# Norms of queries and keys, the gate weight sums, a fold's bank and one tile's copy in a two-layer transformer kernel

## The chip, the cores and the metric

The kernel runs on one core of a Trainium2 chip. The metric is the time of one execution on the device in microseconds (us), as the median of several runs; lower is better. A profile of one execution gives the time of every instruction on the engines: PE is TensorE (matrix products, with PEld for loading its weights), DVE is VectorE, ACT is ScalarE, POOL is GpSimd, and SP issues the transfers (DMA).

## What is computed

A model of two layers on 512 latent tokens and 256 context tokens of width 1024, all in float32. Each layer has a mixer and a gated feed-forward block, and each is modulated by shift, scale and gate vectors that come from two condition vectors. Layer 0 mixes by grouped attention with normed and rotated queries and keys, layer 1 by a gated recurrence. The change lies in layer 0 before attention:

```python
mod_l = (jax.nn.silu(c) @ ada_w[i] + ada_b[i])[:, None, :]       # and mod_c from c_ctx
sh1_l, sc1_l, gt1_l, sh2_l, sc2_l, gt2_l = jnp.split(mod_l, 6, axis=-1)
hn_l = modulate(rms_norm(h, norm_mix_w[i]), sh1_l, sc1_l)         # h * (1 + scale) + shift

def rms_norm(x, w):
    xf = x.astype(jnp.float32)
    y = xf * lax.rsqrt(jnp.mean(xf * xf, axis=-1, keepdims=True) + NORM_EPS)
    return (y * w.astype(jnp.float32)).astype(x.dtype)

def attention_mixer(h_lat, h_ctx, w_qkv, q_norm, k_norm, w_o, rope, with_ctx_out):
    ...
    q_l = apply_axial_rope(queries(h_lat), rope)     # queries: (h @ w_q), rms_norm over the 64 of a head
    k_l, v_l = keys_values(h_lat)                    # keys: rms_norm in the same way
    k_l = apply_axial_rope(k_l, rope)
    k_c, v_c = keys_values(h_ctx)                    # context: normed, not rotated
    ...
    s = jnp.einsum('bkgqd,bksd->bkgqs', q, k) * (HEAD_DIM ** -0.5)   # softmax, times v, times w_o
```

There are 16 query heads and 4 key/value heads of 64. `gt1`, the gate of the mixer (chunk 2 of the six), multiplies the result of attention much later.

## The kernel before, in words

Every product is kept near float32 accuracy by splitting both sides into a high and a low part: `split` (L86 to L95) makes the high part with a cast on ACT (L88) and the low part with a subtraction on DVE (L93), and `mm3` (L114 to L118) does three products for one. Engines run their instructions strictly in the order of the program; the order on each engine is set by a scheduler at build time from the dependences, except for instructions that `pin` keeps in the order of the code.

The part of the program that matters, in order:

**Keys and values.** The normed input lies as eight tiles `xhT` (k = 0 to 7, 128 of the width each, 768 tokens). `kv_group` (L447 to L460) takes each k in turn: a modulate on DVE (L452), the split into `hnh` (ACT) and `hnl` (DVE), then 18 products of 128x512 into three pairs of PSUM banks `kv`. Between these products a filler (`gfill.step`, by the table `KV_STEPS`) puts steps of the modulation products: `ada_group` gives shift and scale in three groups, the last for k = 4 to 7, and `ada_chunk(2, ...)` (L201 to L209) then gives the gate `gt1` from eight blocks `adw` of 128x1024 weights, each one step of four products of 32x256 (`ada_mm`, L185). `ada_put` (L187 to L196) copies the sums to SBUF (`arows`, ACT), transposes them on PE into a bank `pta`, and adds the bias on DVE. The tiles `adw` share six buffers with earlier tiles, so an `adw` is fetched only when a buffer's last reader is done.

**Queries.** For each of four groups g of heads (the loop below `q_first`), two weight tiles `wq` are split (buffers for three high and three low parts), and three tiles of 256 tokens are computed, 48 products of 128x256 each, into one of four `q` banks. I call them tile 0 to tile 11 below. Behind the first three go the three key tiles. `qk_norm_rope` (L512 to L553) then norms and rotates each tile: the square on ACT (L521), the sum on DVE (L524), a scaling (L525), the root on ACT (L526), the reciprocal (L527) and one Newton step of four small operations (L528 to L531) on DVE, the product `qhat` (L533), the rotation on DVE (L543, L552) and POOL (L548), or for the context tile one product with the weight (L537). `k_first` makes two copies `kd` on DVE (L567) and the low part on POOL (L568); `q_first` makes `qd` on DVE (L596) and its low part on POOL (L597). Up to three tiles later PE transposes them into banks of 128x512 (`ptk` L578, `ptq` L603), of which there are three, and ACT copies them out; of the last four 64-row pieces of a key tile DVE copies two (L588). Between the tiles stand eight steps of `ada_chunk(3, ...)`, whose sums lie in a bank of their own, and whose transposes go to one of the three banks.

**Start of attention.** When the last query tile is done, its PSUM pool is closed and the banks become those of the scores `sc` (L656, L657): the first scores wait for the last reader of the `q` banks. PE also transposes the input once more (`rx`, L682) while the softmax of the first tiles begins.

## Time and profile before

| what | value |
|---|---|
| median of three runs (1820.36 to 1823.44) | 1823.32 us |
| the profiled execution's own time | 1821.68 us |
| span of its instructions | 1819.9 us |
| granted TensorE clock, mean over the span | 0.99 |
| first product of the keys and values | 28.24 us |
| first product of the queries (tile 0) | 77.08 us |
| first scores of attention | 179.16 us |

The times in the table's last three rows count from the start of the span. In the rows of the profile, a group of instructions has its line, engine and operation, out<-in by the program's names, the shape and the count; behind the bar stand busy time in us and the mean ns of one, then the idle time of the engine before them and what ended it. Rows of the timeline start with the start and the length in us. A window's row gives the busy time of each engine in that stretch, then the granted clock of PE as a share of full speed.

### The profile page before, as it was taken

To read this page: it belongs to the slowest core of one execution; us is meant where nothing else is said; L and a number is where in the kernel's file an instruction comes from. 1 tells how busy PE (TensorE), PEld (TensorE's weight loads), DVE (VectorE), ACT (ScalarE), POOL (GpSimd) and SP (SyncE) were. 2 spreads that over 40 slices of the span, in tenths; PEclk is the share of its full clock that TensorE was granted. 3 is DMA by queue.
4 is the path that set the end of the run, shared out by engine and by line. 5 is a ranking of instruction groups with operands and counts; after the bars stand their busy time and mean duration, and the time that the engine had idled before them with its cause. 6 is when DMAs were issued, how large, how long until landed. Compare 5 with 4: busy or idle time off the path is not lost.

```text
span 1819.9 us, 30696 instructions
## 1 busy us (share of the span) xinstructions
PE 1755.3 (96%) x11749; PEld 1606.9 (88%) x11749; DVE 1300.5 (71%) x2291; ACT 867.2 (48%) x1768; POOL 637.7 (35%) x583
## 2 busy tenths in 40 slices
PE   8988999999999999999999999999999899999998
PEld 6778678988899999999998999899898799999997
DVE  4587588888888878787865555665747758786764
ACT  4342787676642424333354443343434445554545
POOL 1244254345522304131414333144325544443420
PEclk9999999999999999999999999999999999999999
DMA  8533520002124243445331211222211223333322
GB/s 319 176 105 84 163 79 24 1 24 64 30 87 129 73 137 93 146 133 153 108 116 34 70 59 59 70 82 70 81 56 38 67 59 112 101 106 106 99 60 83
DMA packets 213459, 166.45 MB, mean 91 GB/s; under 512 B 7952, under 2 KB 190400, under 8 KB 213312
## 3 DMA queue, kind: packets, MB, share of 16 engines
q1 hardware_dynamic: 213024, 163.43, 29.2%
q8 instruction: 93, 1.52, 0.4%
q10 hardware_dynamic: 288, 1.05, 0.1%
q14 instruction: 54, 0.44, 0.1%
HBM read 162.36 MB, written 2.10 MB: 90 GB/s over the span
## 4 chain that ended last, share of the span: by engine, by line
PE 78%; DVE 9%; POOL 4%; ACT 4%; issue 2%; DMA 2%; SPq 0%; POOLq 0%; DVEq 0%; ACTq 0%
PE ffo L118 5%; PE ffo L116 5%; PE ffo L117 5%; PE x L116 4%; PE x L117 4%; PE x L118 4%; PE pt L714 3%; PE y L118 2%; PE y L116 2%; PE y L117 2%; PE lv L1643 2%; PE hz L116 2%; PE hz L117 2%; PE hz L118 2%; PE sc L656 2%
## 5 line engine op out<-in xcount | busy, mean ns | idle before, releaser
L1650 POOL TENSOR_TENSOR KD<-KD,tot 128x384 f32<-128x384 f32 x96 | 102.6, 1092 | 82.1 <-ACT kc L1633 78.4
L704 POOL TENSOR_SCALAR pf<-pf,st 128x768 f32<-128x768 f32 (+1 forms) x96 | 73.6, 769 | 128.1 <-DVE st L703 91.6
L687 DVE SCALAR_TENSOR_TENSOR hT<-ffo,modc,hT 128x512 f32<-128x512 f32 (+1 forms) x122 | 78.7, 649 | 48.2 <-PE ffo L118 48.2
L118 PE MATMUL ffo<-gh,wlo_w 128*128 128x512 f32 (+1 forms) x304 | 102.9, 339 | 0.0
L117 PE MATMUL ffo<-gl,whi_w 128*128 128x512 f32 (+1 forms) x304 | 102.4, 337 | 0.0
L116 PE MATMUL ffo<-gh,whi_w 128*128 128x512 f32 (+1 forms) x304 | 102.0, 338 | 0.0
L239 DVE SCALAR_TENSOR_TENSOR adacc<-adw,csil,adacc 128x512 f32<-128x512 f32 x98 | 84.5, 871 | 7.5 <-DMA adw<-in_ada_w_dram 7.4
L93 DVE TENSOR_TENSOR ptl<-pt,pth 128x384 fp32r<-128x384 f32 (+1 forms) x160 | 79.9, 524 | 12.4 <-ACT pth L88 11.2
L88 ACT CAST pth<-pt 128x384 fp32r<-128x384 f32 (+1 forms) x160 | 69.9, 461 | 34.3 <-PE pt L714 22.6
L700 DVE TENSOR_REDUCE st<-sc 128x1 f32<-128x768 f32 (+1 forms) x96 | 74.2, 773 | 15.3 <-PE sc L657 12.6
L702 ACT ACTIVATE pf<-sc,st 128x768 f32<-128x768 f32 (+1 forms) x96 | 73.4, 765 | 19.3 <-DVE st L700 18.4
L1650 DVE TENSOR_TENSOR QD<-QD,tot 128x256 f32<-128x256 f32 x96 | 52.0, 582 | 41.2 <-PE lv L1643 41.1
L1633 ACT COPY kc<-KD 128x256 f32<-128x256 f32 x112 | 43.4, 414 | 75.8 <-PE lv L1643 43.8
L714 PE MATMUL pt<-ident,pf 128*128 128x128 f32 x448 | 72.2, 275 | 5.2 <-DVE ptl L93 3.9
L116 PE MATMUL ffo<-gh,foh 128*128 128x512 f32 (+1 forms) x186 | 71.4, 384 | 0.0
L118 PE MATMUL ffo<-gh,fol 128*128 128x512 f32 (+1 forms) x186 | 70.8, 381 | 0.2 <-DVE fol L93 0.2
L117 PE MATMUL ffo<-gl,foh 128*128 128x512 f32 (+1 forms) x186 | 70.9, 381 | 0.0
L1709 POOL TENSOR_SCALAR oss<-oss 128x4 f32<-128x4 f32 (+1 forms) x9 | 4.7, 524 | 181.8 <-DVE oss L1708 181.7
L1643 PE MATMUL lv<-QD,kc 128*128 128x128 f32 x448 | 63.4, 286 | 4.5 <-DVE QD L1650 2.4
L1643 PEld LDWEIGHTS lv<-QD,kc 128*128 128x128 f32 x448 | 58.7, 192 | 8.8 <-ACT kc L1633 3.8
L714 PEld LDWEIGHTS pt<-ident,pf 128*128 128x128 f32 x448 | 51.2, 140 | 14.4 <-issue 6.4
L117 PEld LDWEIGHTS ffo<-gl,whi_w 128*128 128x128 f32 x304 | 57.4, 189 | 6.9
(1101 smaller groups left out, 6793.9 us busy)
## 6 DMA issues: line engine op xcount, KB each, us to landing
adw<-in_ada_w_dram SPq DMA_DIRECT2D x40, 512.0 KB, 4.7
adw<-in_ada_w_dram SPq DMA_DIRECT2D x80, 256.0 KB, 2.9
raw_hz<-in_hgrn_w_in_dram SPq DMA_DIRECT2D x14, 512.0 KB, 3.8
adr<-in_ada_w_dram SPq DMA_DIRECT2D x16, 256.0 KB, 4.7
adr<-in_ada_w_dram SPq DMA_DIRECT2D x8, 512.0 KB, 7.5
raw_wq<-in_attn_w_qkv_dram SPq DMA_DIRECT2D x8, 512.0 KB, 5.7
raw_wo<-in_attn_w_o_dram SPq DMA_DIRECT2D x8, 512.0 KB, 3.5
raw_hv<-in_hgrn_w_in_dram SPq DMA_DIRECT2D x8, 512.0 KB, 4.9
```

The lines of the kernel that those rows point to most:

```text
L93: m = (eng or DVE).tensor_tensor(lo, src, hi.bitcast(F32), op=ALU.subtract)
L116: PE.matmul(ps, ahi, bhi, start=first, stop=False, **kw)
L117: PE.matmul(ps, ahi, blo, start=False, stop=False, **kw)
L118: PE.matmul(ps, alo, bhi, start=False, stop=last, **kw)
L239: pin(DVE.scalar_tensor_tensor(a, raw, cc, a, op0=ALU.mult, op1=ALU.add))
L687: DVE.scalar_tensor_tensor(hT[o][:, a:e], ps, mcol(layer, ch, o, v), hT[o][:, a:e], op0=ALU.mult, op1=ALU.add)
L700: DVE.tensor_reduce(st3[:, 0:1], ps[:, :nk], op=ALU.max, axis=AX.X, negate=True)
L702: ACT.activation(pf, ps[:, :nk], AF.Exp, bias=st3[:, 0:1], accum_out=st3[:, 1:2])
L704: POOL.tensor_scalar(pf, pf, st3[:, 2:3], 1.0, op0=ALU.mult, op1=ALU.mult)
L714: PE.transpose(pt[:, i * P : (i + 1) * P], pf[:, (i0 + i) * P : (i0 + i + 1) * P], ident)
L1643: PE.matmul(ps[:, cs], kc[:, cs], mv, start=True, stop=True)
L1650: eng.tensor_tensor(view, view, f, op=ALU.mult)
```

## The change

It has six edits, all before attention.

1. **Gate weight sums.** Six of the eight blocks of the gate chunk are no longer multiplied on PE. DVE multiplies each block by the two condition values of its rows and adds it to two sums of 128x1024 (`asum`, twelve operations in fixed order); PE then multiplies the two remaining blocks, and adds each sum over its rows with a column of ones (`pick`), four steps in place of eight.
2. **Modulates.** Those of k = 4 to 7 no longer stand in `kv_group` but in the filler ahead of the sums; those of k = 6 and 7 move from DVE to ACT.
3. **Norm chain.** The scaling is folded into the root (`scale`, `bias`), and the Newton step takes three small operations for four, its constant -0.5/64 being folded into the norm weights (one more small POOL operation). Five DVE operations a tile are left of seven up to the factor `ss`, the sum and the reciprocal included.
4. **Keys.** The two copies `kd` and the two 64-row copies out of PSUM move from DVE to ACT.
5. **Fold.** The transposes of chunk 3 go to the free half of the bank that holds its sums.
6. **Last query tile.** DVE copies it from PSUM to SBUF (`qraw`) first; the norm chain reads the copy.

On SP the last two `adw` of the gate chunk come to stand behind one and two small transfers (`rows2`), ahead of which they stood, since their buffers are now released by the sums on DVE.

```diff
+ADA_SUMS = 6
...
-    def ada_put(pa, rows, dst, bias, nch, nk):
+    def ada_put(pa, rows, dst, bias, nch, nk, pt=None):
...
-        pt = bank("pta")
+        pt = bank("pta") if pt is None else pt
...
     def ada_chunk(ch, pa, rows, load):
+        pt = None if pa is None else pa[:, 256:512]
...
+    def ada_shared(ch, nsum):
+
+        pa = bank("pa")[:, 0:256]
+        sums = [stp.tile([P, D], F32, name=f"asum{v}") for v in range(2)]
...
+        for step in range(KT + 1):
+            if step < KT:
+                raws.append(xx_tile(f"adw{ch}{step}"))
+                dma(raws[-1], ada_w[0, step * P : (step + 1) * P, ch * D : (ch + 1) * D])
+            k = step - 1
+            if k >= nsum:
+                products(raws[k], cpad[:, k], k == nsum, False)
+            for v in range(2 if 0 <= k < nsum else 0):
+                cc = csil[:, v, k : k + 1]
+                if k == 0:
+                    pin(DVE.tensor_scalar(sums[v], raws[k], cc, None, op0=ALU.mult))
+                else:
+                    pin(DVE.scalar_tensor_tensor(sums[v], raws[k], cc, sums[v], op0=ALU.mult, op1=ALU.add))
+            yield
+        for v in range(2):
+            products(sums[v], pick[:, v], False, v == 1)
...
+    def first_modulate(k):
+        for v, a, e in SP2:
+            xs, sc, sh = xhT[k][:, a:e], a_c0[:, k, v : v + 1], mcol(0, 0, k, v)
+            if k < KT - 2:
+                DVE.tensor_scalar(xs, xs, sc, sh, op0=ALU.mult, op1=ALU.add)
+            else:
+                ACT.activation(xs, xs, AF.Identity, bias=sh, scale=sc)
+        split(hn_hi[k], hn_lo[k], xhT[k])
+
+    def last_modulates():
+        for k in range(KT // 2, KT):
+            first_modulate(k)
+        yield from ada_shared(2, ADA_SUMS)
...
-        DVE.tensor_scalar(ss, ss, 1.0 / HD, EPS, op0=ALU.mult, op1=ALU.add)
-        ACT.activation(sr, ss, AF.Sqrt)
+        ACT.activation(sr, ss, AF.Sqrt, bias=epst, scale=1.0 / HD)
         DVE.reciprocal(sr, sr)
         DVE.tensor_tensor(sa, sr, sr, op=ALU.mult)
-        DVE.tensor_tensor(sa, sa, ss, op=ALU.mult)
-        DVE.tensor_scalar(sa, sa, -0.5, 1.5, op0=ALU.mult, op1=ALU.add)
-        DVE.tensor_tensor(ss, sr, sa, op=ALU.mult)
+        DVE.scalar_tensor_tensor(sa, ss, HD * EPS, sa, op0=ALU.add, op1=ALU.mult)
+        DVE.scalar_tensor_tensor(ss, sa, -3.0 * HD, sr, op0=ALU.add, op1=ALU.mult)
...
-            DVE.tensor_copy(kd[:, :, :, i].rearrange("p t h d -> p (t h) d"), r.rearrange("p t h d -> p (t h) d"))
+            ACT.copy(kd[:, :, :, i].rearrange("p t h d -> p (t h) d"), r.rearrange("p t h d -> p (t h) d"))
...
-                    DVE.tensor_copy(dst[HD:P], pg[rows])
+                    ACT.copy(dst[HD:P], pg[rows])
...
+        if g == KVH - 1 and tp == 2:
+            raw = qst.tile([P, 512], F32, tag="kraw", bufs=2, name="qraw")
+            DVE.tensor_copy(raw, ps)
+            ps = raw
```

The order on three engines shows what moves; line numbers behind the edits are higher in the changed kernel (L93 is L94 there, L452 is L466). First DVE, from the split of k = 4 (`hnl_99`) to the first splits of the query weights. Before:

```order
L93 TENSOR_TENSOR hnl_99<-xhT_291,hnh_91 128x768
L93 TENSOR_TENSOR wlo_wkv_504<-raw_wkv_502,whi_wkv_503 128x1024
L93 TENSOR_TENSOR hnl_100<-xhT_300,hnh_92 128x768
L452 TENSOR_SCALAR xhT_309<-xhT_309,a_c_202,modc_82 128x256
L452 TENSOR_SCALAR xhT_318<-xhT_318,a_c_202,modc_82 128x512
L452 TENSOR_SCALAR xhT_318<-xhT_318,a_c_202,modc_82 128x256
L93 TENSOR_TENSOR hnl_101<-xhT_309,hnh_93 128x768
L93 TENSOR_TENSOR hnl_102<-xhT_318,hnh_94 128x768
L93 TENSOR_TENSOR wlo_wkv_572<-raw_wkv_570,whi_wkv_571 128x1024
L195 TENSOR_TENSOR modc_82<-pta,cols_80 128x16
L93 TENSOR_TENSOR wlo_wq_749<-raw_wq_747,whi_wq_748 128x1024
```

Of the changed kernel, with two pairs of sums left out at its end:

```order
L94 TENSOR_TENSOR hnl_99<-xhT_295,hnh_91 128x768
L94 TENSOR_TENSOR hnl_100<-xhT_304,hnh_92 128x768
L94 TENSOR_TENSOR hnl_101<-xhT_313,hnh_93 128x768
L94 TENSOR_TENSOR wlo_wkv_522<-raw_wkv_520,whi_wkv_521 128x1024
L94 TENSOR_TENSOR hnl_102<-xhT_322,hnh_94 128x768
L453 TENSOR_SCALAR asum_516<-adw_518,csil 128x1024
L453 TENSOR_SCALAR asum_517<-adw_518,csil 128x1024
L455 SCALAR_TENSOR_TENSOR asum_516<-adw_526,csil,asum_516 128x1024
L455 SCALAR_TENSOR_TENSOR asum_517<-adw_526,csil,asum_517 128x1024
L455 SCALAR_TENSOR_TENSOR asum_516<-adw_552,csil,asum_516 128x1024
L455 SCALAR_TENSOR_TENSOR asum_517<-adw_552,csil,asum_517 128x1024
L94 TENSOR_TENSOR wlo_wkv_584<-raw_wkv_582,whi_wkv_583 128x1024
```

The low weights of k = 4 and 5 (`wlo_wkv_522`) now stand behind three input splits, and the low weights of k = 6 and 7 behind six of the twelve sums.

Second ACT, from the copies of the first key tile out of PSUM (`kT`) to the root of tile 1 (its square reads `q_872`, in the changed kernel `q_871`). Before:

```order
L582 CAST kT<-ptk 128x2x256 x2
L587 CAST kT<-ptk 64x2x256
L521 ACTIVATE qrot<-q_872 128x512
L587 CAST kT<-ptk 64x2x256
L88 CAST whi_wq_1139<-raw_wq_1138 128x1024
L526 ACTIVATE ss<-ss 128x8
```

Of the changed kernel:

```order
L630 CAST kT<-ptk 128x2x256 x2
L635 CAST kT<-ptk 64x2x256
L636 CAST kT<-ptk 64x2x256
L635 CAST kT<-ptk 64x2x256
L636 CAST kT<-ptk 64x2x256
L615 CAST kd<-qrot 128x8x64 x2
L570 ACTIVATE qrot<-q_871 128x512
L89 CAST whi_wq_1130<-raw_wq_1129 128x1024
L575 ACTIVATE ss<-ss,epst 128x8
```

The square of tile 1 now stands behind the two `kd` copies of the second key tile.

Third PE at the start of attention, behind the transposes of tile 8 and 9. Before:

```order
L656 MATMUL sc<-kT,qT_705 128x512
L657 MATMUL sc<-kT,qT_705 128x512
L656 MATMUL sc<-kT,qT_705 128x256
L657 MATMUL sc<-kT,qT_705 128x256
L603 MATMUL ptq<-ident,qd 128x128 x8
L682 MATMUL rx_2040<-ident,hT_2004 128x128 x2
L603 MATMUL ptq<-ident,qd 128x128 x8
L682 MATMUL rx_2040<-ident,hT_2004 128x128 x4
L185 MATMUL pa<-adw_2120,cpad 32x256 x4
```

Of the changed kernel:

```order
L708 MATMUL sc<-kT,qT_707 128x512
L709 MATMUL sc<-kT,qT_707 128x512
L708 MATMUL sc<-kT,qT_707 128x256
L709 MATMUL sc<-kT,qT_707 128x256
L655 MATMUL ptq<-ident,qd 128x128 x8
L734 MATMUL rx_2014<-ident,hT_1978 128x128 x6
L708 MATMUL sc<-kT,qT_707 128x512
L709 MATMUL sc<-kT,qT_707 128x512
L708 MATMUL sc<-kT,qT_707 128x256
L709 MATMUL sc<-kT,qT_707 128x256
L655 MATMUL ptq<-ident,qd 128x128 x8
L186 MATMUL pa<-adw_2094,cpad 32x256 x4
```

The transposes of the last query tile (the second `ptq`) now stand behind all of `rx` and a second set of scores.

More of the change, by code (lines that the diff above doesn't have):

```diff
@@ L208, in ada_chunk @@
             yield
-        ada_put(pa, rows(), modc[0][:, ch : ch + 1], ada_bias(0, ch, 1), 1, KT)
+        ada_put(pa, rows(), modc[0][:, ch : ch + 1], ada_bias(0, ch, 1), 1, KT, pt)
     def ada_acc(layer, ch, nv, fp, wide):
@@ L423, with products @@
         gfill.add(ada_group(*g_))
-    gfill.add(ada_chunk(2, None, lambda: stp.tile([P, 256], F32, tag="arows", bufs=2, name="arows2"), xx_tile))
+    pick = stp.tile([P, 2, 32], F32, name="pick")
+    POOL.memset(pick, 0.0)
+    for v in range(2):
+        POOL.memset(pick[:, v, v : v + 1], 1.0)
+    def ada_shared(ch, nsum):
+        pa = bank("pa")[:, 0:256]
+        sums = [stp.tile([P, D], F32, name=f"asum{v}") for v in range(2)]
+        def products(m, col, start, stop):
+            m4 = m.rearrange("p (b j n) -> p b j n", b=2, j=4)
+            for j in range(4):
+                PE.matmul(pa[32 * j : 32 * (j + 1)], col, m4[:, :, j], start=start, stop=stop)
+        raws = []
+        for step in range(KT + 1):
[12 more added lines that the diff above has]
+            yield
+        for v in range(2):
+            products(sums[v], pick[:, v], False, v == 1)
+        rows = stp.tile([P, 256], F32, tag="arows", bufs=2, name="arows2")
+        ada_put(pa, rows, modc[0][:, ch : ch + 1], ada_bias(0, ch, 1), 1, KT)
+    def first_modulate(k):
[10 more added lines that the diff above has]
+        yield from ada_shared(2, ADA_SUMS)
+    gfill.add(last_modulates())
     gfill.step(4)
@@ L450, in kv_group @@
             k = k0 + j
-            for v, a, e in SP2:
-                DVE.tensor_scalar(xhT[k][:, a:e], xhT[k][:, a:e], a_c0[:, k, v : v + 1], mcol(0, 0, k, v),
-                                  op0=ALU.mult, op1=ALU.add)
-            split(hn_hi[k], hn_lo[k], xhT[k])
+            if k < KT // 2:
+                first_modulate(k)
             for t in range(NT):
@@ L496 @@
         dma(w, wsrc.to_broadcast([P, HD]))
[L497 to L498 removed]
+        POOL.tensor_scalar(w, w, -0.5 * sc / HD, 1.0, op0=ALU.mult, op1=ALU.mult)
         cw = qst.tile([P, NLT, HD], F32, name=f"cw{nm}")
```

2 lines of the change are left out of this document (removed).

## The prediction

> **What bounds the kernel now.** I read the page first:
>
> ```profile
> PE 1755.3 (96%) x11749; PEld 1606.9 (88%) x11749; DVE 1300.5 (71%) x2291; ACT 867.2 (48%) x1768; POOL 637.7 (35%) x583
> PE 78%; DVE 9%; POOL 4%; ACT 4%; issue 2%; DMA 2%; SPq 0%; POOLq 0%; DVEq 0%; ACTq 0%
> ```
>
> The first row says that PE is busy nearly always, the second that of the chain which ends last 22% is not PE. All six edits lie in the first 185 us, so I read only that stage: where PE waits from 77 to 185 us, and what clock PE was granted (windows; behind the five engines stand the clock, the DMA share and GB/s).
>
> ```profile
> PE q L117 <- DVE wlo_wq L93: 3.7, 2, 2.4
> PE sc L656 <- DVE qhat L533: 3.5, 1, 3.5
> PE pta L193 <- ACT kT L582: 3.3, 1, 3.3
> ```
>
> ```profile
> 118.00:122.00 4.00, 0.70 (x7) 0.46 (x5) 2.64 (x8) 1.28 (x4) 2.12 (x2) 0.89 0.50 191
> 122.00:128.00 6.00, 6.00 (x29) 6.00 (x30) 4.88 (x9) 1.05 (x3) 3.36 (x5) 0.50 0.01 1
> 133.00:136.00 3.00, 0.58 (x5) 0.48 (x5) 2.79 (x4) 0.32 (x1) 1.67 (x2) 1.00 0.00 0
> 175.00:179.00 4.00, 0.63 (x6) 0.39 (x4) 3.35 (x10) 1.71 (x5) 1.26 (x1) 1.00 0.98 273
> 179.00:185.00 6.00, 5.84 (x36) 4.93 (x36) 2.78 (x5) 2.87 (x5) 0.00 (x0) 0.72 1.19 290
> ```
>
> ```profile
> 122.64 0.41 PE L117 MATMUL q<-wlo_wq,hnh 128*128 128x256 f32 x1
> 122.85 0.41 PE L118 MATMUL q<-whi_wq,hnl 128*128 128x256 f32 x1
> ```
>
> The waits add up to 10.5 us, and they cost more than they last: behind the wait of 3.3 us (118 to 122) PE ran 6 us at clock 0.50, with products of 256 columns every 0.21 us (the two rows) instead of every 0.117, which loses about 2.5 us (26 of them), behind that of 3.5 us it had 0.72 (a loss of 6 x 0.28 = 1.7 us); behind that of 2.4 us (133 to 136) it lost nothing. Everything behind 185 us keeps its order up to some swaps, so I take it that a gain there stays to the end.
>
> **Part 1, keys and values (to 77 us).** On PE one step of the gate chunk costs this:
>
> ```profile
> 51.44 0.40 PE L118 MATMUL kv<-whi_wkv,hnl 128*128 128x512 f32 x1
> 51.76 0.64 PE L185 MATMUL pa<-adw,cpad 128*32 128x256 f32 x8
> 52.33 0.50 PE L116 MATMUL kv<-whi_wkv,hnh 128*128 128x512 f32 x1
> ...
> 55.95 0.50 PE L116 MATMUL kv<-whi_wkv,hnh 128*128 128x512 f32 x1
> ...
> 77.08 0.36 PE L116 MATMUL q<-whi_wq,hnh 128*128 128x256 f32 x1 [0.61 <-DVE cols L474]
> ```
>
> Products of 128x512 follow each other every 0.23 us; across a step it is 0.89, so a step costs 0.66 us, and four fewer save 2.6. Against it stand two new waits. First, four steps stood between 48 and 55.95, where k = 4 begins; without them PE comes there at 53.3. But ACT now does the modulate of k = 6, three casts and that of k = 7 before it casts the weights of k = 4, and DVE their low part behind three input splits. Their durations:
>
> ```profile
> L88 ACT CAST hnh<-xhT 128x768 fp32r<-128x768 f32 x8 | 6.7, 834 | 6.7 <-DVE xhT L452 6.7
> L88 ACT CAST whi_wkv<-raw_wkv 128x1024 fp32r<-128x1024 f32 x4 | 4.2, 1048 | 1.5 <-DMA raw_wkv<-in_attn_w_qkv_dram 1.4
> L93 DVE TENSOR_TENSOR wlo_wkv<-raw_wkv,whi_wkv 128x1024 fp32r<-128x1024 f32 x4 | 4.9, 1224 | 1.0 <-ACT whi_wkv L88 1.0
> L387 DVE TENSOR_SCALAR xx<-xx,rs 128x1024 f32<-128x1024 f32 x6 | 4.5, 754 | 11.3 <-ACT junk L384 7.7 <-POOL rs L386 2.9 <-DMA adr<-in_ada_w_dram 0.7
> L239 DVE SCALAR_TENSOR_TENSOR adacc<-adw,csil,adacc x98: 735/746/1785, 516.8 to 883.4; 128x512 f32<-128x512 f32 x98
> ```
>
> From 48.5, five of 0.8 and one of 1.05 give 53.5, the low part 54.8: PE loses 1.1 us there. Second, DVE's sums: from 55.6 two operations like the fourth row (1.4), ten of 1024 like the last row, whose 0.74 for 512 grows to about 1.25, and one weight split: 55.6 + 1.4 + 12.5 + 1.1 = 70.6. PE wants the first sum at 69.7. POOL's tables fall into the same time: they wait for transfers that SP issues behind the last `adw`.
>
> ```profile
> 45.05 7.74 SPq L205 DMA_DIRECT2D adw<-in_ada_w_dram  x4
> ...
> 59.04 0.73 POOL L501 TENSOR_TENSOR cwk<-ropec,wk 128x256 f32<-128x256 f32 x1 [43.99 <-DMA wk<-in_attn_k_norm_dram]
> 59.73 1.17 POOL L507 TENSOR_TENSOR swk<-ropes,wk 128x64 f32<-128x64 f32 x4
> ```
>
> There the last `adw` went out at 52.8 and POOL began 6.2 us later. Now the last `adw` waits for the second pair of sums (59.4), so the tables begin at about 65.6, and the first query weights, queued behind them on SP, come 6 us later too, still ahead of 70. Does POOL hold up DVE? Yes, by these rows of two places:
>
> ```profile
> 148.39 1.31 POOL L597 TENSOR_TENSOR qd<-qrot,qd 128x512 fp32r<-128x512 f32 x1 [1.34 <-DVE qd L596]
> ...
> 516.39 1.62 POOL L1147 TENSOR_TENSOR raw_('w', 4, 1)_5983<-raw_('w', 4, 1)_5983 128x512 f32<-128x512 f32 x1
> ```
>
> ```profile
> 148.94 0.79 DVE L525 TENSOR_SCALAR ss<-ss 128x8 f32<-128x8 f32 x1
> ...
> 516.79 1.78 DVE L239 SCALAR_TENSOR_TENSOR adacc<-adw,csil,adacc 128x512 f32<-128x512 f32 x1
> ```
>
> ```profile
> L525 DVE TENSOR_SCALAR ss<-ss x15: 164/570/792, 76.0 to 176.3; 128x8 f32<-128x8 f32 x15
> ```
>
> The small DVE operation, 0.16 us at the least (the last row has its least, median and longest in ns), ended when POOL's did (149.7); the sum took 1.04 us more than its median. So I let the tables add 1.5 of their 4.3 us (twice 0.73 + 1.17 + 0.25), and the sums end at 72.1, the next to last at 70.8: PE waits 1.1 us. Sum: -2.6 + 1.1 + 1.1, and the wait of 0.61 for `cols` (the 77.08 row) shrinks since DVE is nearer: tile 0 starts at 75.8, **-1.3**. Bounds: -3 (no wait) to +8 (the slow rival below).
>
> **Part 2, tiles 0 to 5.** The shorter chain takes 0.2 us from each tile, and the scaling, 0.16 us or up to 0.79 where POOL holds it (its row above). But `kd` on ACT adds a latency: behind the rotation of the second key tile come two casts (1.1) and the square of tile 1 (0.6), where DVE now sums that tile at once. So DVE, which is 0.5 us ahead at the second key tile, is level again at tile 1:
>
> ```profile
> 102.85 0.69 DVE L533 TENSOR_TENSOR qhat<-q,ss 128x512 f32<-128x512 f32 x1
> ...
> 130.16 0.69 DVE L533 TENSOR_TENSOR qhat<-q,ss 128x512 f32<-128x512 f32 x1
> ...
> 134.25 1.22 DVE L93 TENSOR_TENSOR wlo_wq<-raw_wq,whi_wq 128x1024 fp32r<-128x1024 f32 x1
> ```
>
> I get 102.6 for the first row (tile 1), 125.5 for the second (tile 4): four chains between them at 0.7 each, and the copies `kd` and `kT` that leave DVE there, some 2 us (an estimate from 0.69 for 512 elements: two such, and two quicker). The weight split (third row) then stands at 129.7. PE, 0.4 us ahead at tile 3, comes to the fold at 118.0 (118.7 before: the 0.70 us of the 118 to 122 row):
>
> ```profile
> 116.04 0.38 ACT L190 COPY arows<-pa 128x256 f32<-128x256 f32 x1
> ...
> 120.72 0.21 ACT L526 ACTIVATE ss<-ss 128x8 f32<-128x8 f32 x1 [3.80 <-DVE ss L525]
> ```
>
> The sums were copied at 116.4, but the bank came free only behind a copy that ACT had queued behind the root at 120.72. With its own bank the fold waits for the copy alone, which now stands behind that root (118.1): 118.4. Tile 5 starts at 118.8 for 122.28 and, at full clock (48 products at 0.117), ends at 124.5.
>
> **Part 3, tiles 6 to 11.** A transpose (0.9) and 12 products (1.4) later, at 126.8, PE needs the weights of the 134.25 row; before it came there at 135.52 less 2.42. So PE is 6.3 us earlier, DVE 4.5:
>
> ```profile
> 135.52 0.39 PE L117 MATMUL q<-wlo_wq,hnh 128*128 128x256 f32 x1 [2.42 <-DVE wlo_wq L93]
> ```
>
> So this wait grows from 2.42 to some 4 us, and PE goes on at 130.8, **-4.7**. The two waits of 3.3 us or more were followed by a slow clock, so I charge 2.5 us for it. [...] Behind it DVE, which saves 0.7 us on each of three tiles of a group, no longer falls behind PE, so the second wait for weights (3.7 less 2.4 in the first table) goes: -1.3. At the end of tile 11: -4.7 + 2.5 - 1.3 = **-3.5**.
>
> **Part 4, start of attention.**
>
> ```profile
> 173.72 1.91 PE L603 MATMUL ptq<-ident,qd 128*128 128x128 f32 x16
> 179.16 0.80 PE L656 MATMUL sc<-kT,qT 128*128 128x512 f32 x1 [3.52 <-DVE qhat L533]
> ...
> 182.67 1.18 PE L603 MATMUL ptq<-ident,qd 128*128 128x128 f32 x8
> ```
>
> ```profile
> 178.41 0.69 DVE L533 TENSOR_TENSOR qhat<-q,ss 128x512 f32<-128x512 f32 x1
> ```
>
> The scores waited for `qhat` as last reader of the bank. The copy (0.7 us, as `qhat`) ends some 0.8 us behind tile 11 and inside the 1.91 us of transposes: the wait and its clock go, -5.2. The last tile's chain gets later by the copy, and the last `ptq` then waits about 1.3 us, with `rx` and the second scores ahead of it to fill in: **-3.9**. What then is late next is the first `rx`, whose input SP fetches when tile 11's inputs are free; that lies in the same 1.3 us.
>
> **Sum:** -3.5 - 3.9 = -7.4 us. The profiled execution took 1821.7, 1.6 less than the median of the three runs; 7.4 less is 1814.3 by the one and 1815.9 by the other, and I say 1815.0, from 1822.4 half way between. Of a measurement of this kernel 0.2% (3.6 us) can be told from no change.
>
> **The rivals.**
> - *The clock holds in tile 6.* [...] Chance 0.30.
> - *ACT takes DVE's place.* ACT executes in order, and `kd`, `kT` and the fold's copy now stand around roots that wait for DVE. If each key tile loses 1.5 us, the fold's wait and its slow clock stay and DVE gains nothing by tile 6; left are 1.3 and 3.9: -5.2, 1817.2. Chance 0.15.
> - *The copy does not free the banks,* because another reader is last, and the fold finds another wait: -1, 1821.4. The trace names the reader, but not who is second. Chance 0.07.
> - *The sums are late (slower).* If a sum ran at half rate, 1024 would take 0.53 x 2 us more per 1024 (0.53 us is 1.22 less 0.69, two lengths of one kind of operation): ten cost 10.5, PE waits over 3.3 us for them and loses 2.5 by the clock, tile 0 starts at 88.8, +11.7. The later gains (7.4 - 1.3 = 6.1, and 2.5 more, since PE no longer comes early to tile 6) take 8.6 back: +3.1, 1825; it decides from 10 us of delay. Against it: 0.74 us for 512 is not half rate. [...] Chance 0.06.
>
> **How the numbers follow.** Forecast 0.42, and the rivals as above. The range, 1809.5 to 1820.0, takes in the first two rivals, 3 us below the one and above the other for a DVE chain that is wrong by 0.3 us a tile; it leaves out the last two. Faster by over 0.2%: 0.42 + 0.30 + most of 0.15, so 0.83; within: 0.11; slower: 0.06.
>
> **What would show it.** Right: tile 0 some 1.3 us earlier with waits for `wlo_wkv` and `asum`; no wait of `pta` over 1 us and clock 1.00 in tile 5; a wait of 3 to 4 us in tile 6 with clock near 0.5 behind it; no wait of the first scores. Wrong: sums of over 1.5 us each, PE idle for `asum` over 3 us, or a new wait behind 185 us as long as the gain.

## The result and the profile after

The changed kernel takes 1812.51 us (median of 6 executions, 1808.9 to 1814.47); the kernel before took 1822.62 in the executions beside it. The ratio is 0.9946 with a 95% interval of 0.9934 to 0.9958: it is faster by about 10 us, where 7.4 were forecast. The profiled execution took 1813.7 us, with a span of 1811.9, which is 8.0 less than before. From the page, the busy times and the chain that ended last:

```profile
PE 1750.5 (97%) x11717; PEld 1605.3 (89%) x11717; DVE 1299.8 (72%) x2258; ACT 874.9 (48%) x1784; POOL 644.6 (36%) x587
PE 77%; DVE 6%; ACT 4%; POOL 4%; issue 2%; DMA 1%; POOLq 0%; DVEq 0%; ACTq 0%
```

PE has 4.8 us less work (four gate steps and less time at half clock), DVE's busy time is the same, though four of its operations per key tile have gone to ACT and its norm chains are shorter: the sums took their place. DVE's share of the chain fell from 9 to 6%. The longest waits of PE from 26 to 185 us (in total, times, longest), and one of 0.6 that is used below:

```profile
PE q L118 <- DVE wlo_wq L94: 3.5, 1, 3.5
PE ptk L626 <- ACT qT L658: 2.5, 1, 2.5
PE kv L117 <- ACT whi_wkv L89: 1.0, 1, 1.0
PE sc L708 <- ACT hT L735: 0.9, 1, 0.9
...
PE ptq L655 <- DVE qd L649: 0.6, 1, 0.6
```

The long waits of before (3.7, 3.5 and 3.3) have become one of 3.53 for tile 6's weights; the fold's and the first scores' are gone, and the key transposes wait 2.5 in place of 1.5. The same windows as before, and one more (busy times of the five engines, then the clock, the DMA share and GB/s):

```profile
118.00:122.00 4.00, 3.83 (x34) 3.60 (x33) 3.08 (x8) 3.61 (x8) 2.70 (x4) 1.00 0.97 347
122.00:128.00 6.00, 5.42 (x47) 5.22 (x46) 4.25 (x11) 4.20 (x8) 3.37 (x6) 1.00 0.03 13
128.00:136.00 8.00, 5.06 (x30) 5.06 (x31) 5.79 (x10) 0.45 (x2) 3.91 (x4) 0.79 0.42 121
175.00:179.00 4.00, 3.12 (x40) 2.04 (x42) 2.79 (x4) 2.14 (x3) 0.00 (x0) 1.00 1.19 295
179.00:185.00 6.00, 5.13 (x39) 3.54 (x34) 1.51 (x5) 4.94 (x11) 1.86 (x3) 1.00 1.09 379
```

The half clock has moved from tile 5 (122 to 128) to tile 6 (128 to 136 has a mean of 0.79), and the one at the start of attention is gone. PE in order of time, at tile 0, the fold, tile 6, and the start of attention:

```profile
76.10 0.38 PE L117 MATMUL q<-whi_wq,hnh 128*128 128x256 f32 x1 [0.61 <-DVE cols L524]
...
118.97 0.44 PE L194 MATMUL pa<-ident,arows 128*128 128x128 f32 x2 [0.17 <-ACT arows L191]
...
130.94 0.58 PE L118 MATMUL q<-wlo_wq,hnh 128*128 128x256 f32 x1 [3.53 <-DVE wlo_wq L94]
...
169.08 1.91 PE L655 MATMUL ptq<-ident,qd 128*128 128x128 f32 x16
170.74 0.47 PE L708 MATMUL sc<-kT,qT 128*128 128x512 f32 x1
```

Against before, tile 0 is 0.98 us earlier, tile 6 goes on 4.58 earlier, tile 11's transposes come 4.64 earlier and the first scores 8.4. DVE of the kernel after, then DVE's first key `qhat` of the kernel before:

```profile
63.68 7.26 DVE L455 SCALAR_TENSOR_TENSOR asum<-adw,csil,asum 128x1024 f32<-128x1024 f32 x6
...
72.95 1.30 DVE L94 TENSOR_TENSOR wlo_wq<-raw_wq,whi_wq 128x1024 fp32r<-128x1024 f32 x1
...
74.29 1.65 DVE L94 TENSOR_TENSOR wlo_wq<-raw_wq,whi_wq 128x1024 fp32r<-128x1024 f32 x1
79.98 0.69 DVE L581 TENSOR_TENSOR qhat<-kraw,ss 128x512 f32<-128x512 f32 x1
...
103.11 0.69 DVE L581 TENSOR_TENSOR qhat<-q,ss 128x512 f32<-128x512 f32 x1
...
125.59 0.69 DVE L581 TENSOR_TENSOR qhat<-q,ss 128x512 f32<-128x512 f32 x1
129.67 1.22 DVE L94 TENSOR_TENSOR wlo_wq<-raw_wq,whi_wq 128x1024 fp32r<-128x1024 f32 x1
```

```profile
78.72 0.69 DVE L533 TENSOR_TENSOR qhat<-kraw,ss 128x512 f32<-128x512 f32 x1
```

DVE reaches its first `qhat` 1.26 us later than before and yet splits tile 6's second weights 4.58 us earlier (129.67 against 134.25). Three points in time follow the stage through every kernel below. **A** is DVE's first key `qhat`, **B** is DVE's split of tile 6's second weights, and **C** is the last product `po` of attention, which comes behind all that the change touches. C is the second number of such a row (first and last start), here of the kernel after:

```profile
L777 PE MATMUL po<-pth,vv x224: 274/282/390, 189.6 to 418.2; 128*128 128x256 f32 x112
```

### The profile page after: what moved, and what is told of

It reads as the page before. It is cut to its first block, busy times and chain, and to the rows that moved or that the text cites. A ratio compares the mean times of both kernels' runs of the same rounds, so it can differ in the third digit from the quotient of the medians.

```text
span 1811.9 us, 30618 instructions
## 1 busy us (share of the span) xinstructions
PE 1750.5 (97%) x11717; PEld 1605.3 (89%) x11717; DVE 1299.8 (72%) x2258; ACT 874.9 (48%) x1784; POOL 644.6 (36%) x587
## 4 chain that ended last, share of the span: by engine, by line
PE 77%; DVE 6%; ACT 4%; POOL 4%; issue 2%; DMA 1%; POOLq 0%; DVEq 0%; ACTq 0%
PE ffo L119 5%; PE ffo L117 5%; PE ffo L118 5%; PE x L117 4%; PE x L118 4%; PE x L119 4%; PE pt L766 3%; PE lv L1695 3%; PE y L119 2%; PE y L117 2%; PE y L118 2%; PE hz L117 2%; PE hz L118 2%; PE hz L119 2%; PE sc L708 1%
## 5 line engine op out<-in xcount | busy, mean ns | idle before, releaser
L119 PE MATMUL ffo<-gh,wlo_w 128*128 128x512 f32 (+1 forms) x304 | 102.6, 338 | 0.0
L94 DVE TENSOR_TENSOR ptl<-pt,pth 128x384 fp32r<-128x384 f32 (+1 forms) x160 | 79.8, 523 | 12.5 <-ACT pth L89 11.3
L766 PE MATMUL pt<-ident,pf 128*128 128x128 f32 x448 | 72.1, 275 | 5.2 <-DVE ptl L94 3.9
```

The source lines that it names most:

```text
L94: m = (eng or DVE).tensor_tensor(lo, src, hi.bitcast(F32), op=ALU.subtract)
L119: PE.matmul(ps, alo, bhi, start=False, stop=last, **kw)
L766: PE.transpose(pt[:, i * P : (i + 1) * P], pf[:, (i0 + i) * P : (i0 + i + 1) * P], ident)
```

## The experiments

Every ratio is to the kernel before, timed beside it. One execution of each kernel was profiled (us):

| kernel | A | B | B - A | C | C - B | ratio, 95% interval |
|---|---|---|---|---|---|---|
| before | 78.72 | 134.25 | 55.53 | 426.4 | 292.2 | |
| after | 79.98 | 129.67 | 49.69 | 418.2 | 288.5 | 0.9946 [0.9934, 0.9958] |
| b_chain | 77.04 | 129.18 | 52.14 | 417.8 | 288.6 | 0.9962 [0.9949, 0.9974] |
| b_fold | 78.00 | 133.56 | 55.56 | 425.9 | 292.3 | 1.0005 [0.9996, 1.0014] |
| b_qraw | 78.23 | 133.74 | 55.51 | 423.8 | 290.1 | 0.9994 [0.9985, 1.0003] |
| a_oldchain | 80.46 | 131.22 | 50.76 | 420.8 | 289.6 | 0.9978 [0.9969, 0.9986] |
| a_kdve | 79.03 | 130.98 | 51.95 | 418.0 | 287.0 | 0.9956 [0.9942, 0.9971] |
| a_nosums | 78.08 | 128.36 | 50.28 | 416.0 | 287.6 | 0.9945 [0.9931, 0.9959] |
| a_fold3 | 79.70 | 129.38 | 49.68 | 416.2 | 286.8 | 0.9948 [0.9936, 0.9960] |
| a_noqraw | 79.02 | 128.74 | 49.72 | 416.2 | 287.5 | 0.9952 [0.9940, 0.9965] |
| a_warm | 78.69 | 128.38 | 49.69 | 417.6 | 289.2 | 0.9954 [0.9942, 0.9966] |
| a_hifirst | 77.73 | 127.42 | 49.69 | 415.4 | 288.0 | 0.9949 [0.9935, 0.9964] |
| n_kdlate2 | 77.47 | 128.10 | 50.63 | 415.0 | 286.9 | 0.9953 [0.9939, 0.9966] |
| n_hifirst2 | 77.75 | 128.08 | 50.33 | 413.1 | 285.0 | 0.9932 [0.9918, 0.9945] |

B - A hardly depends on the execution: the five kernels that share the code up to tile 6, but for the fold's bank in a_fold3 (after, a_fold3, a_noqraw, a_warm, a_hifirst), give 49.68 to 49.72, whatever clock PE had there. A does: in the same five it lies between 77.73 and 79.98. So does the time behind C, where the kernels have the same instructions: it took between 1390.8 us (b_chain) and 1395.2 us (a_oldchain), so that up to 4.4 us between two profiled executions are none of the change's; in before and after it is the same to 0.2 us. My theory was that DVE's chains, with the ACT and POOL steps between them, set when PE goes on in tile 6, so that PE's own waits and clock up to there cost nothing. The rival was that the waits removed add up.

### The fold's bank: b_fold and a_fold3

b_fold is the kernel before with this edit alone, a_fold3 the kernel after without it:

```diff
-        pt = None if pa is None else pa[:, 256:512]
+        pt = None
```

> The kernel before, with one edit alone: the fold of the gate weights in the free half of its own bank. Theory (DVE and ACT set when tile 6 goes on; PE is only early or late for it): the wait of 3.30 us goes and PE runs tile 5 at full clock, but DVE's split of the second weights for tile 6 still starts some 57.2 us behind the first product of tile 0 (134.25 against 77.08), so PE waits there for 5 to 8 us in place of 2.42 and goes on within 1 us of where it did; the slow clock, which lay ahead of that wait and was hidden by it, then falls behind it and isn't: -1 to +2 us against the kernel before. Rival (the waits add up): 3.3 us and most of the 2.5 us of slow clock are gained, -4 to -6 us.

PE's waits in b_fold from 77 to 185 us, the three longest:

```profile
PE q L117 <- DVE wlo_wq L93: 5.1, 1, 5.1
PE sc L657 <- DVE qhat L534: 3.5, 1, 3.5
PE q L116 <- ACT whi_wq L88: 1.8, 1, 1.8
```

The fold's 3.3 us are gone, and the weights of tile 6 take 5.1 + 1.8 in place of 2.42. B - A and C - B are those of before to 0.1 us, and the ratio is 1.0005. The rival's -4 to -6 us is excluded.

> The kernel after, with the fold put back into a bank of the ring of three. Theory: the bank was worth 3.3 us and a slow clock only to the kernel before, since there DVE and ACT freed the ring late; here the copies of the key transposes stand on ACT one behind the other, the first frees its bank near 119.9 us, so the fold starts near 120.0 instead of 118.97, tile 5 ends 1 us later, and the wait of tile 6 for wlo_wq shrinks from 3.53 to some 2.5 us, since DVE still splits these weights at 129.7: PE goes on at 130.9 as before, and with the shorter wait the half clock behind it may go too. Time 0 to -1.5 us against the kernel after (1811 to 1812.5). Rival (the waits removed add up): the wait of 3.3 us and the clock of 2.5 us come back, +3 to +6 us (1816 to 1818).

The profiled a_fold3 shows why the clock matters as little as the bank. Its windows at tile 1:

```profile
100.00:102.00 2.00, 0.55 (x3) 0.55 (x4) 1.93 (x5) 2.00 (x4) 0.00 (x0) 0.50 0.00 0
102.00:104.00 2.00, 2.00 (x15) 1.41 (x17) 1.86 (x5) 1.92 (x4) 0.37 (x1) 0.50 0.81 256
```

and its longest waits from 26 to 185 us:

```profile
PE ptk L626 <- ACT qT L658: 2.5, 1, 2.5
PE q L118 <- DVE wlo_wq L94: 1.4, 1, 1.4
```

Here the half clock fell behind the wait of the key transposes, PE came to the fold 1.8 us later (120.76 against 118.97) and found the bank free; the wait of tile 6 shrank from 3.53 to 1.44 us, and B - A stayed. Because PE was late, this execution does not show whether the ring's bank would have held up the fold of a PE at full clock; the ratio says that it makes no difference that can be measured.

### The norm chain: b_chain and a_oldchain

b_chain is the kernel before with this edit alone; a_oldchain is the kernel after with the reverse of it. The scaling of the weights goes with it.

```diff
-        DVE.tensor_scalar(ss, ss, 1.0 / HD, EPS, op0=ALU.mult, op1=ALU.add)
-        ACT.activation(sr, ss, AF.Sqrt)
+        ACT.activation(sr, ss, AF.Sqrt, bias=epst, scale=1.0 / HD)
...
-        DVE.tensor_tensor(sa, sa, ss, op=ALU.mult)
-        DVE.tensor_scalar(sa, sa, -0.5, 1.5, op0=ALU.mult, op1=ALU.add)
-        DVE.tensor_tensor(ss, sr, sa, op=ALU.mult)
+        DVE.scalar_tensor_tensor(sa, ss, HD * EPS, sa, op0=ALU.add, op1=ALU.mult)
+        DVE.scalar_tensor_tensor(ss, sa, -3.0 * HD, sr, op0=ALU.add, op1=ALU.mult)
```

> The kernel after, with the norm chain of before (two more small operations of DVE and the scaling in each chain, and the weights as they were). Theory: up to tile 6's weights eight chains with three small operations more each, 0.16 to 0.23 us and their gaps of 0.05: 0.6 us a chain, 4 to 5 us of DVE work; DVE stands idle for some of it anyway, so the split of tile 6's second weights starts 56 to 58 us behind tile 0's first product instead of 53.6, PE goes on 2.5 to 4.5 us later, and a wait at tile 9 of 1 us comes back: +3 to +5 us against the kernel after. Rival (the chain's small operations hide in DVE's idle time, the gain came from kd and kT): less than +1.5 us, the split within 1 us of 53.6.

> The kernel before, with one edit alone: the short norm chain and its weights. Theory (DVE's chains set the pace of the whole stage, and undoing the chain in the kernel after cost some 4 us): the split of tile 6's second weights starts 53.5 to 54.7 us behind DVE's first key qhat instead of 55.5, tile 11's qhat 42 to 43.3 us behind that split instead of 44.2, and the last transposes come 3 to 4.5 us earlier, though the fold still waits for its bank and the first scores for qhat: -3 to -4.5 us against the kernel before. Rival (the shorter chain needs kd on ACT as well to be worth anything): 0 to -1.5 us.

Undone in the kernel after, it costs 5.8 us (0.9978 against 0.9946), of which the table shows 1.1 ahead of B and some 2.8 behind it (289.6 against 286.8 of a_fold3, both without a half clock behind B); the profiles don't show where the other 1.9 are. So the part ahead of B was smaller than I expected (the split came 54.25 us behind tile 0 instead of 56 to 58), and the part behind it larger. Alone in the kernel before it gains 6.9 us (4.7 to 9.3), half as much again as my upper figure of 4.5, with B - A down by 3.4 and C - B by 3.6. PE's waits in b_chain from 77 to 185 us, the longest, and the fold's:

```profile
PE q L117 <- DVE wlo_wq L93: 4.0, 1, 4.0
PE ptk L575 <- ACT qT L603: 1.9, 1, 1.9
PE sc L653 <- DVE qhat L530: 1.8, 1, 1.8
...
PE pta L193 <- ACT kT L579: 0.6, 1, 0.6
```

Neither the fold's bank nor the copy was touched, yet the fold's wait fell from 3.3 to 0.6 us (the root that stands on ACT ahead of the copy that frees the bank comes at 116.72 us instead of 120.72; in the kernel before ACT stood idle for 3.80 us up to that root, though PE had written the copy's input by 118.64), the first scores' from 3.52 to 1.8, and the second wait for weights is gone. C is 417.8, where all six edits together have 418.2; b_chain has the earlier A, and from A to C it takes 340.8 us, the kernel after 338.2 and the kernel before 347.7.

The chain has lost two DVE operations of seven, not three as the expectation of a_oldchain counts, and they cost more than their least time. The scaling alone, 0.16 us at the least, took 0.54 us in the mean of its fifteen: in eleven of them it ended 0.03 us behind an operation of POOL. From 75 to 180 us the small operations behind the sum, without the reciprocal, were 19.5 us of DVE before and are 8.9 in b_chain; with all that falls into that time DVE is busy for 75.6 us instead of 82.9.

### The casts on ACT: a_kdve

```diff
-            ACT.copy(kd[:, :, :, i].rearrange("p t h d -> p (t h) d"), r.rearrange("p t h d -> p (t h) d"))
+            DVE.tensor_copy(kd[:, :, :, i].rearrange("p t h d -> p (t h) d"), r.rearrange("p t h d -> p (t h) d"))
...
-                    ACT.copy(dst[HD:P], pg[rows])
+                    DVE.tensor_copy(dst[HD:P], pg[rows])
```

> The kernel after, with the casts kd and the second copies of kT back on DVE. DVE then has per key tile 1.1 us of casts and 1.2 us of copies more, 6.9 us over the three; ACT has as much less, and the latencies in which DVE stood idle behind it (1.82 and 2.24 us) shrink. Theory: DVE's idle time of tiles 0 to 5 takes in about half of it, the split for tile 6 comes 2 to 4 us later (132 to 134) and PE with it; time +1.5 to +4 us (1814 to 1816.5). Rival (the move to ACT costs as much as it frees): tile 1's and tile 4's qhat stand within 0.7 us of the kernel after, and the time within 1 us of it.

B - A grows by 2.26 us, in the theory's range of 2 to 4, but the ratio, 0.9956 with an interval of 0.9942 to 0.9971, cannot be told from that of the kernel after. The three longest waits of PE in a_kdve from 77 to 185 us show that the two forms share the same stall differently:

```profile
PE q L118 <- DVE wlo_wq L94: 2.7, 1, 2.7
PE ptk L626 <- DVE kT L636: 2.1, 1, 2.1
PE ptk L626 <- ACT qT L658: 1.9, 1, 1.9
```

### The copy of the last query tile: b_qraw and a_noqraw

```diff
+        if g == KVH - 1 and tp == 2:
+            raw = qst.tile([P, 512], F32, tag="kraw", bufs=2, name="qraw")
+            DVE.tensor_copy(raw, ps)
+            ps = raw
```

> The kernel before, with one edit alone: the last query tile copied out of PSUM by DVE ahead of its norm chain. Theory: nothing behind it makes up for a wait at the start of attention, so the 3.52 us of the first scores and the slow clock behind them (1.7) go, less some 1.3 us of new waits of the last transposes: -3.5 to -5 us against the kernel before, all of it behind 175 us. Rival: the first scores wait for another reader of the banks, or the last transposes get later by as much: 0 to -1.5 us.

> The kernel after, without the copy of the last query tile out of PSUM. Theory (DVE's chains set the end of this stage, the copy only moves the wait): DVE's qhat of tile 11 starts 0.7 us earlier than with the copy, some 41.5 us behind the split of tile 6's second weights (42.1 with it), and PE's first scores wait for it by 2 to 3 us; the last transposes, which with the copy wait for the same chain, then come only 0.5 to 1.5 us later: +0.5 to +1.5 us against the kernel after, and 1 to 1.7 more where the clock falls behind that wait. Rival (the term of the prediction): the wait of 3.5 us and its clock come back in full, +3.5 to +5 us.

b_qraw misses what I expected, and its rival was right: the first scores wait 0.6 us instead of 3.52, and C - B falls by 2.1, but the ratio is 0.9994, between -2.7 and +0.5 us. In a_noqraw the time, 1.1 us above the kernel after by the ratios, would fit the theory but cannot be told from no change, and the wait is shorter than the 2 to 3 us I had. C - B is 287.5, 0.7 above that of a_fold3, and this is its only long wait at the start of attention (of 100 to 185 us), with the clock at 1.00 behind it:

```profile
PE sc L704 <- DVE qhat L581: 1.8, 1, 1.8
```

With the copy PE has 0.9 for the second scores, 0.6 for the last transposes and 0.9 for `rx` there. The copy exchanges one wait for DVE's chain for three small ones, one for that chain (`qd`) and two for ACT (`hT`, `pf`); in the profiles it is worth 0 to 0.7 us in the kernel after (C - B of a_nosums and a_fold3, which have it), and by the times not more than 2.7 in the kernel before. The prediction's term of 3.9 is excluded there; in the kernel after the times leave it open, but the profile of a_noqraw does not show it.

### The gate sums: a_nosums

The gate chunk goes back to PE for all eight steps, and all modulates to DVE at their old place:

```diff
-    gfill.add(last_modulates())
+    gfill.add(ada_chunk(2, None, lambda: stp.tile([P, 256], F32, tag="arows", bufs=2, name="arows2"), xx_tile))
...
-            if k < KT // 2:
-                first_modulate(k)
+            first_modulate(k)
```

> The kernel after, with the gate chunk of the first modulation back on PE for all eight steps and all the modulates back where they were on DVE. Theory: four steps of 0.66 us more on PE up to 77 us, less the waits for whi_wkv, wlo_wkv and the cast hnh (1.0 + 0.3 + 0.5) that go: tile 0's first product stands at 76.8 to 77.5 instead of 75 to 76.1, and everything behind it keeps its distance (the split of tile 6's second weights 53.6 us behind it): +0.8 to +1.8 us. Rival: the tables and the first query weights, which SP then gets earlier, let DVE and POOL start the key chains earlier, and nothing is lost: within 0.5 us of the kernel after.

The rival is right: the ratio is 0.9945. Tile 0 does start later without the sums, at 76.25 us in the mean of three kernels (76.56 in a_nosums), where the six with the sums and the short chain have 75.38 (74.55 to 76.10). But A comes earlier, at 77.77 against 79.03 in the same means: DVE's first `qhat` stands 1.5 us behind tile 0 in the three kernels without the sums, and 3.2 to 3.9 us behind it in the six with them. DVE in a_nosums is free long before the query weights come, and has split them at 72.7 us:

```profile
70.23 0.17 DVE L196 TENSOR_TENSOR modc<-pta,cols 128x16 f32<-128x16 f32 x1 [13.06 <-PE pta L194]
70.32 2.35 DVE L94 TENSOR_TENSOR wlo_wq<-raw_wq,whi_wq 128x1024 fp32r<-128x1024 f32 x2
...
78.08 0.69 DVE L580 TENSOR_TENSOR qhat<-kraw,ss 128x512 f32<-128x512 f32 x1
```

In the kernel after DVE begins with them at 72.95, but not because its sums last so long: they end at 70.94, and DVE then stands idle for 1.41 us. ACT and POOL are late, each in its rows (first ACT, then POOL):

```profile
70.30 1.05 ACT L89 CAST whi_wq<-raw_wq 128x1024 fp32r<-128x1024 f32 x1 [14.22 <-DMA raw_wq<-in_attn_w_qkv_dram]
74.89 0.63 ACT L570 ACTIVATE qrot<-kraw 128x512 f32<-128x512 f32 x1 [1.36 <-POOL cwq L550]
```

```profile
66.15 4.89 POOL L547 TENSOR_SCALAR wk<-wk 128x64 f32<-128x64 f32 x1 [51.04 <-DMA wk<-in_attn_k_norm_dram]
72.94 0.24 POOL L547 TENSOR_SCALAR wq<-wq 128x64 f32<-128x64 f32 x1
```

SP issues the query weights at 63.0 us instead of 56.0, behind the last `adw`, which wait for the sums; ACT's first cast of them waits for that transfer, and the copies of keys and values stand behind the cast. And POOL's first operation for the tables, which takes 0.24 us for `wq` and in a_nosums, took 4.89 and ended at 71.04, 0.1 us behind the last sum. In the four kernels in which it was held like this (after, a_fold3, a_noqraw, a_warm) the square of the first chain then waits 1.4 to 1.5 us for the tables, and `qhat` is 3.9 us behind tile 0; in a_kdve and a_hifirst it was not held, and it is 3.2. So the sums give PE some 0.9 us ahead of tile 0 and cost the first chain more, and behind tile 0 the chain is waited for.

### What would have to change: a_warm, a_hifirst, n_kdlate2, n_hifirst2

a_warm puts 30 products that nobody reads into tile 6, ahead of the first that needs the second weights:

```diff
+                    if g == 2 and tp == 0 and tt == 0 and k == 4:
+                        for i in range(30):
+                            PE.matmul(apsum[:, 0:256], hn_hi[0][:, 0:P], ws[0][0][:, 0], start=True, stop=True)
```

> The kernel after, with 30 products of 128x256 that nobody reads (3.4 us of PE at full clock) put into tile 6 just ahead of the first product that needs the second weights. Theory: the wait is set by DVE's split at 129.7, so PE still goes on at 130.9 to 131.1, and only the clock changes: 1.00 in place of 0.50 from 131 to 134.2, 15 products at 0.117 instead of 0.213 us, -1.5 us at the end of tile 6 and at the end of the kernel (about 1811 against 1812.5; more where the half clock would last longer). Rival 1: the end of tile 11 is set by DVE's chain and not by PE, so the gain is eaten by a new wait before the first scores: 0. Rival 2: the half clock isn't due to the idle stretch: it comes anyway, 0.

This is inconclusive as to the clock. In the profiled execution the half clock fell at tile 1 (some 98 to 107 us), PE came to the filler late, and it ran into the time in which the weights were there:

```profile
128.02 3.66 PE L692 MATMUL pa<-whi_wq,hnh 128*128 128x256 f32 x30
```

The weights were split by 129.6, the filler ended at 131.7. It cost PE 2 us, and C - B is 289.2 instead of 286.8 to 287.5: here a delay of PE behind B reaches C.

a_hifirst gives PE real work for that time. Tile 6's products are put in another order (in this form the second half's start falls while the sum of the first half is open in the same bank, and the output is off by 0.42, relative; n_hifirst2 below has one start for both and the model's output; the instructions are the same):

```diff
+            if g == 2 and tp == 0:
+                for tt in range(2):
+                    for k in range(KT):
+                        part(tt, k, 0, 0, start=(k == 0))
+                        part(tt, k, 1, 0)
+                        if k < 4:
+                            part(tt, k, 0, 1)
+                for tt in range(2):
+                    for k in range(4, KT):
+                        part(tt, k, 0, 1, stop=(k == KT - 1))
```

> The kernel after, with tile 6's products in another order: all those that need no low part of the second weights first (28 more, 3.3 us), then the eight that do. Theory: PE needs the low part near 130.3 instead of 127.3, DVE splits it at 129.7 as before and it is there at 130.9, so the wait shrinks from 3.53 to about 0.6 us and the clock stays at 1.00: -2.9 and -1.5, PE -4.4 us at the end of tile 6; DVE's chain of the tiles behind (some 6.4 us a tile at the most, where PE takes 6.5) then has little room, so between half and all of it arrives: 1808 to 1810.5. Rival: DVE sets the pace of tiles 7 to 11 too, waits of tiles 9 and 10 or of the first scores take its place: 1811.5 to 1812.5.

The wait of tile 6 is gone, and in its place PE waits in tile 9:

```profile
147.65 0.39 PE L118 MATMUL q<-wlo_wq,hnh 128*128 128x256 f32 x1 [1.91 <-DVE wlo_wq L94]
```

with half clock behind it, so that C - B is 288.0 and the ratio 0.9949. The rival was right for this kernel, as far as the times can tell.

n_kdlate2 (without the sums) lets the query tile's square and root go ahead of the casts `kd` on ACT:

```diff
+        begun[tp] = norm_parts(ps.rearrange("p (t h d) -> p t h d", t=2, d=HD), tp, "q")
+        next(begun[tp])
         kd = qst.tile([P, 2, KVH, 2, HD], F32R, tag="sp", bufs=3, name="kd")
```

> The kernel after without the gate sums (as a_nosums), and with ACT's work of the three key tiles in another order: the square and the root of the query tile stand ahead of the casts kd of the same key tile, where they wait for nothing but PE, so that DVE's next sum need not wait for a rotation that POOL or DVE itself has still to end. Theory (the latency of kd on ACT is what stands in DVE's way in tiles 1 and 2: 2.43 us ahead of the sum of tile 1, 2.23 ahead of the reciprocal of tile 2): of these 4.6 us, 2.5 to 4.5 go, so the split of tile 6's second weights starts 46 to 48 us behind DVE's first key qhat instead of 50.3, PE waits there for 0 to 1 us instead of 2.41, and the time is 1.5 to 2.5 us below a_nosums (ratio about 0.9933). Rival (POOL's rotations and its lock set DVE's pace): the split stays within 0.7 us of 50.3, no gain.

Tile 1's `qhat` comes at 97.39 us where a_nosums has it at 101.79, but B - A is 50.63, as the rival had it, though not for its reason (by POOL's lock it means such rows as two of this run: small operations of DVE took 0.85 and 1.24 us and ended 0.02 us behind one of POOL). PE's two longest waits from 77 to 185 us:

```profile
PE ptk L642 <- ACT qT L674: 3.5, 1, 3.5
PE q L118 <- DVE wlo_wq L94: 0.9, 1, 0.9
```

The copies `qT` that free the banks now stand later on ACT, and PE's wait for them grows from 1.8 to 3.5 us; the one of tile 6 shrinks from 2.41 to 0.94. The sum of the two is the same 4.2 to 4.4 us, and DVE gains nothing by tile 6. What holds it up instead is not settled: ACT now waits 4.02 us for PE's products ahead of the square at 118.99, and DVE 2.52 us for the root behind it.

n_hifirst2 is a_nosums with the order of a_hifirst in tiles 6 and 9, and one start and one stop for both halves of the bank (the lines that differ from a_hifirst):

```diff
-            if g == 2 and tp == 0:
+            if g >= 2 and tp == 0:
...
-                        part(tt, k, 0, 0, start=(k == 0))
+                        part(tt, k, 0, 0, start=(tt == 0 and k == 0))
...
-                        part(tt, k, 0, 1, stop=(k == KT - 1))
+                        part(tt, k, 0, 1, stop=(tt == 1 and k == KT - 1))
```

> The kernel after without the gate sums (as a_nosums), and in tiles 6 and 9 all products that need no low part of the second weights first, as in a_hifirst, but with one start for both halves of the bank. Theory (a wait of PE for DVE's splits in this stage ends only where PE has other work for it; DVE itself stands idle for PE's tiles by 0.3 to 1 us each from tile 7 on): the waits of tile 6 (2.41 us in a_nosums) and of tile 9 (1.91 in a_hifirst) are filled, no half clock falls there, and the last transposes come 1 to 2.4 us earlier, measured from the split of tile 6's second weights (44 to 44.7 us behind it instead of 45.7 for the start of the last one): ratio 0.9935 or a little below. Rival (DVE's chains set the pace to the end): the last transposes wait for tile 11's chain by as much as PE gains, 45.3 to 45.9 us behind the split, no gain.

Its waits from 100 to 185 us, the longest:

```profile
PE ptk L625 <- ACT qT L657: 1.8, 1, 1.8
PE sc L722 <- ACT hT L749: 0.9, 1, 0.9
PE rx L748 <- ACT pf L768: 0.9, 1, 0.9
PE ptq L654 <- DVE qd L648: 0.6, 1, 0.6
```

No product waits for weights any more. The last transpose starts 43.8 us behind B (45.7 in a_nosums), a little sooner than the theory had it, C - B is 285.0, the smallest of all, and the ratio 0.9932 (0.9918 to 0.9945), 1809.1 us. It is the fastest kernel of the study; against a_nosums C - B shows where 2.6 us come from, but the intervals overlap with that of a_nosums (0.9931 to 0.9959) and of the kernel after (0.9934 to 0.9958), so the times alone don't show the gain.

## Why the prediction was right, and where it was not

**Part 1, keys and values.** Tile 0 was to start at 75.8 and started at 76.10, 0.98 us earlier instead of 1.3, but partly by luck. The terms of the sum, -2.6 + 1.1 + 1.1, come to -0.4, and to -1.0 with all of the wait for `cols`, which did not shrink (0.61 us as before). The new waits at k = 4 were 1.0 us for the high part and 0.3 for the low part (1.1 foreseen) and 0.5 for the cast `hnh`, which was not foreseen; the wait of 1.1 us for the sums did not come. The sums take 1.28 us each (estimate 1.25) and end at 70.94 instead of 72.1: POOL's tables were to hold them up by 1.5 us, and instead the sums held POOL up (its 4.89 us above). And the step "tile 0 starts 1.3 us earlier" has no consequence, since behind it DVE is waited for, not PE, and DVE's first `qhat` comes 1.26 us later. a_nosums shows that edits 1 and 2 are worth nothing that can be measured.

**Part 2, tiles 0 to 5.** `qhat` of tile 1 came at 103.11 (102.6 foreseen), of tile 4 at 125.59 (125.5), the split at 129.67 (129.7), the fold at 118.97 (118.4). That the split fell on the forecast is luck in part: from A to B the stage became 5.8 us shorter, where the split was to come 4.5 us earlier, and A came 1.3 us later. The step that the fold's gain only makes PE early for tile 6 is confirmed by b_fold. I gave the shorter chain 2.8 us up to the split; alone it takes 3.4 from B - A (b_chain), beside the other edits 1.1 (a_oldchain). And I gave the fold's wait to its bank, whereas the chain alone takes most of it.

**Part 3, tiles 6 to 11.** PE went on at 130.94 (130.8 foreseen), and the wait was 3.53 us (some 4). The clock fell behind it, but 15 products at 0.213 us lost 1.4 us instead of 2.5. That is the 1.1 us by which tile 11's transposes came earlier than foreseen (4.64 against 3.5). The second wait for weights went, as foreseen, and with the old chain one of 1.26 us comes back in tile 9 (a_oldchain).

**Part 4, start of attention.** Behind tile 11's transposes another 3.6 us were gained by C (8.2 in all), against 3.9 foreseen. The size is right and the cause is wrong: this is the step that failed. The copy was to take the scores' wait and its slow clock away, 5.2 us for 1.3 of new waits; b_qraw (2.1 us by C - B, 1.1 by the ratio) and a_noqraw show that it moves most of the wait. What shortens it is the shorter chain: in b_chain tile 11's `qhat` starts 42.2 us behind B instead of 44.2, PE's transposes keep their distance from B (39.3 for 39.5), and the first scores wait 1.79 us without the copy, as in a_noqraw, and with no slow clock behind them.

**The sum.** The profiled execution lost 8.0 us where I had 7.4. Of the 2.5 us between 1815.0 and 1812.5 this is 0.6; another 0.7 is that 1815.0 was counted from 1822.4 (half way is 1822.5) and not from the profiled 1821.7, and 1.2 that the median of after lies so far below its profiled execution. The first rival, the clock that holds in tile 6 (1812.5), is the case of other executions: the profiled after and b_chain had the half clock in tile 6, where it reaches the end, while a_fold3, a_noqraw, a_nosums and others had it at tile 1, where tile 6's wait hides it. That the six times of the kernel after lie in two groups (1808.9 to 1811.4 and 1813.7 to 1814.5) fits this, but stays argued: there is no profile of the kernel after from the lower group, by C - B the half clock in tile 6 costs 0.9 to 1.7 us (288.5 against 286.8 to 287.6 in a_fold3, a_kdve, a_noqraw and a_nosums), less than the groups are apart, and behind C executions differ by up to 4.4. That the median fell on the rival's 1812.5 does not speak for it, since the profiled execution did have the half clock.

**Where the gain is from.** Some 6 to 7 of the 10 us are the norm chain's (5.8 when it is undone, 6.9 alone). The other five edits together gain some 4.0 us without it (a_oldchain, 0.9978), but no run shows by which of them: `kd` and `kT` on ACT bring B forward by 2.3 us, which the times cannot separate, and they were not tried alone in the kernel before; fold, copy and sums are each within their measurement of nothing.

## What to carry to other kernels

When an engine waits at several places for the same slower chain of other engines, its waits are one quantity: removing one of them lengthens the next (in b_fold 3.3 us went at the fold and 4.5 came in tile 6), and what shortens the whole is a shorter chain, or, by the profile of n_hifirst2 alone, other work in the wait. Measure from a fixed point of the chain to the next such point (here 49.7 us in five kernels) rather than add up the waits. Small operations in such a chain count though their engine is idle a fifth of the time (75 to 180 us before): fifteen chains lost two operations each, 10.6 us of small operations in all, and some 7 us arrived at the end. Price them by their mean in the trace and not by their least (0.54 and 0.16 us for the scaling).
